# Attention scores in a hybrid decoder layer: q's high and low parts on the two row halves, two passes per head in place of three

## The chip, the core and the metric

The kernel runs on one core of one Trainium2 chip. The metric is the device time of one execution in microseconds (us); the time given for a kernel is the median of its runs. Rows of a trace come from one profiled execution, in us from the start of its span, and durations of single instructions are in ns where the row says so.

The engines are named as in the profile: PE is TensorE's matmul pipe and PEld its weight load, DVE is VectorE, ACT is ScalarE, POOL is GpSimd, SP is SyncE, which issues the weight loads from memory.

## What is computed

One decoder layer on 512 tokens of width 1024: a feed-forward block, a mixer of two branches on the same input (sliding-window attention with sinks, and a state-space scan), and a second feed-forward block, each followed by a layer norm. All in float32. The change touches the scores of the attention branch alone:

```python
qb = q.reshape(b, nb, ATTN_BLOCK, N_KV_HEADS, rep, HEAD_DIM)      # 4 blocks of 128 tokens, 4 x 4 heads of 64
kk, vv = with_prev(kb), with_prev(vb)                             # the block before, and the block itself
scores = jnp.einsum("bnqgrd,bnkgd->bngrqk", qb, kk).astype(jnp.float32) * (HEAD_DIM ** -0.5)
...
probs = jax.nn.softmax(jnp.concatenate([scores, sink], axis=-1), axis=-1)[..., :-1]
out = jnp.einsum("bngrqk,bnkgd->bnqgrd", probs.astype(v.dtype), vv)
```

The first block of tokens has no block before it, so it has 128 keys; the other three have 256.

## The kernel before

**Products of split numbers.** Nearly every matrix product is made of three TensorE passes. An operand is split into a high part (a copy rounded to fp32r, made by ACT) and a low part (the remainder, made by DVE from the original and the high part); `split_act` on lines 142 to 146 does this for activations and `split_w` on lines 96 to 102 for weights. `mm3` on lines 123 to 126 then runs high by high, high by low and low by high into one PSUM accumulator.

**Attention stage.** It lies between 400 and 560 us of the span. A list of 20 main tiles runs on PE: six tiles of q (`q_tile(2)` to `q_tile(7)`; the first two stand ahead of the list), six tiles of the scan's inputs, eight gate tiles. Each main tile is a product over 1024 inputs, 24 passes of 512 columns on the whole 128 x 128 array. `weave` (lines 374 to 392) puts one step of attention behind each main tile, which holds the scores of one unit, the values of the unit two before it and the turning of the probabilities of the unit one before it. A unit is one group of four heads (one key head) by one block of 128 tokens, so there are 16 units: 12 have 256 keys and 4 (the first block of each group) have 128.

**Scores.** `q_tile(i)` leaves two heads in one tile, head 0 on rows 0 to 63 and head 1 on rows 64 to 127, the high part and the low part side by side in the free dimension. `k_tile` (lines 436 to 444) puts high and low parts of each key head on both row halves, so that a head of q finds its keys on its own rows. In `scores`, line 476 runs `mm3` for each of the four heads on 64 rows: heads 0 and 2 on rows 0 to 63, heads 1 and 3 on rows 64 to 127, 12 passes a unit. The two halves write to two PSUM tiles (`pss`).

**Behind the scores.** DVE adds the band mask and takes the row maximum (line 478), ACT takes the exponential (line 485), DVE scales (line 491). PE turns the probabilities (line 500) and ACT and DVE split them (`pt`), PE multiplies by v (`values`).

**Order.** The order on each engine is made when the kernel is built: a scheduler places instructions by priority in the order of the code, and `issue_after` keeps attention's instructions behind the last pass of the main tile (`cur["mm"]`). Four PSUM buffers serve the main tiles (`acc`) and four the rest (`sm`). The q tiles have two buffers (`qT`, line 449): the tile of group 2 can be written only when the scores of group 0 are done, that of group 3 when those of group 1 are.

Of the kernel before, what the change touches and what calls it, by code (L numbers as in the profile page):

```python
# [12 lines left out]
ALU = mybir.AluOpType  # L13

P = 128
# [24 lines left out]
def hybrid_layer(  # L40
# [5 lines left out]
    nc = tc.nc  # L46
# [9 lines left out]
    def acc(name="acc"):  # L56
        return psum.tile([P, 512], F32, tag="acc", name=name)

    def sm(name="sm"):
        return psum.tile([P, 512], F32, tag="sm", name=name)  # L60

    def f(ap):
        return ap.bitcast(F32)
# [51 lines left out]
    def load_w(*srcs, pool=None, own=0):  # L115
        return split_w(*fetch_w(*srcs), pool=pool, own=own)

    def wcols(w, r0, nk, c0, n):
        return w[r0:r0 + nk * P, c0:c0 + n].rearrange("(k p) c -> p k c", p=P)

    cur = {}

    def mm3(ps, lh, ll, rh, rl, start, stop):
        nc.tensor.matmul(ps, lh, rh, start=start, stop=False)  # L124
        nc.tensor.matmul(ps, lh, rl, start=False, stop=False)  # L125
        cur["mm"] = nc.tensor.matmul(ps, ll, rh, start=False, stop=stop)  # L126

    def gemm_T(w, act, kk, col=0, ps=None, tok=slice(0, SEQ)):

        ps = ps or acc()  # L130
        wh, wl = w
        n = len(kk)
        for i, k in enumerate(kk):
            mm3(ps[:, tok], wh[:, i, col:col + P], wl[:, i, col:col + P], act[:, k, 0, tok], act[:, k, 1, tok], i == 0, i == n - 1)
        return ps
# [6 lines left out]
    def split_act(dst, ps):  # L142

        a = nc.scalar.copy(dst[0], ps)  # L144
        b = nc.vector.tensor_tensor(dst[1], ps, f(dst[0]), ALU.subtract)  # L145
        return a.ins, b.ins
# [115 lines left out]
    with tc.tile_pool(name="start", bufs=1) as pool:  # L262
# [7 lines left out]
        for k in range(8):  # L270
            ps = sm()
# [33 lines left out]
    with tc.tile_pool(name="mix", bufs=1) as mix:  # L305
# [89 lines left out]
        with tc.tile_pool(name="attn", bufs=1) as ap:  # L395
# [4 lines left out]
            for t in range(NT):  # L400
                ps = acc("vdt")
                tok = slice(t * P, (t + 1) * P)
# [29 lines left out]
            kT = ap.tile([P, NKV, 2, SEQ], F32R, name="kT")  # L432
            aT = ap.tile([P, 8, 2, SEQ], F32R, name="aT")
            qTs = {}
# [11 lines left out]
            def q_tile(i):  # L446
                g = i // 2
                if i % 2 == 0:
                    qTs[g] = ap.tile([P, 2, 2, SEQ], F32R, name="qT", bufs=2)
                ps = gemm_T(load_w(wcols(w_in, 0, 8, i * P, P)), xT, range(8))  # L450
                split_act((qTs[g][:, i % 2, 0], qTs[g][:, i % 2, 1]), ps)

            def attention():
                units = [(g, t) for g in range(NKV) for t in range(NT)]
                st = {}
                smls = ap.tile([P, 4, 8, 4], F32, name="smls")
                sinkB = smls[:, 3].rearrange("p a b -> p (a b)")[:, :16]
                nc.gpsimd.dma_start(sinkB, sinks[0].partition_broadcast(P))

                def scores(u):  # L460
                    g, t = u
                    tok = slice(t * P, (t + 1) * P)
                    nk = 1 if t == 0 else 2
                    ks = slice((t + 1 - nk) * P, (t + 1) * P)
                    pr = ap.tile([P, 4, 2 * P], F32, name="pr", bufs=2)
                    s3 = 4 * g + t
                    sml = smls[:, s3 % 3]
                    mx, nm, rs, es, rc = (sml[:, i] for i in range(5))
                    sink = sinkB[:, 4 * g:4 * g + 4]
                    bandv = band.rearrange("p a b -> p (a b)")[:, (2 - nk) * P:]  # L470
                    pss = [sm().rearrange("p (a b) -> p a b", a=2) for _ in range(2)]
                    for i in range(2):
                        for hh in range(2):
                            pp = slice(hh * 64, hh * 64 + 64)
                            q_, k_ = qTs[g][pp, i, :, tok], kT[pp, g, :, ks]
                            mm3(pss[hh][:, i, :nk * P], q_[:, 0], q_[:, 1], k_[:, 0], k_[:, 1], True, True)
                    for h in range(4):
                        nc.vector.tensor_tensor_reduce(
                            out=pr[:, h, :nk * P], in0=pss[h % 2][:, h // 2, :nk * P], in1=bandv, op0=ALU.add, op1=ALU.max,
                            scale=1.0, scalar=MASKED, accum_out=mx[:, h:h + 1])  # L480
                    nc.vector.scalar_tensor_tensor(nm, mx, 0.125, sink, ALU.mult, ALU.max)
                    nc.vector.tensor_tensor(es, sink, nm, ALU.subtract)
                    nc.vector.tensor_scalar_mul(nm, nm, -1.0)
                    for h in range(4):
                        nc.scalar.activation(pr[:, h, :nk * P], pr[:, h, :nk * P], AF.Exp, bias=nm[:, h:h + 1],  # L485
                                             scale=0.125, accum_out=rs[:, h:h + 1])
                    nc.scalar.activation(es, es, AF.Exp)
                    nc.vector.tensor_tensor(rc, rs, es, ALU.add)
                    nc.vector.reciprocal(rc, rc)
                    for h in range(4):  # L490
                        nc.vector.tensor_scalar_mul(pr[:, h, :nk * P], pr[:, h, :nk * P], rc[:, h:h + 1])
                    st[u] = (pr, nk)

                def turn(u):
                    pr, nk = st[u]
                    pts = []
                    for b in range(nk):
                        ps = sm()
                        for h in range(4):
                            nc.tensor.transpose(ps[:, h * P:(h + 1) * P], pr[:, h, b * P:(b + 1) * P], ident)  # L500
                        pt = ap.tile([P, 2, 4 * P], F32R, name="pt", bufs=3)
                        split_act((pt[:, 0], pt[:, 1]), ps)
                        pts.append(pt)
                    st[u] = pts

                def values(u):
                    g, t = u
                    pts = st.pop(u)
                    ps = sm()
                    nk = len(pts)  # L510
                    for b in range(nk):
                        v_ = vs[:, t + 1 - nk + b, :, g * HD:(g + 1) * HD]
                        mm3(ps[:HD], v_[:, 0], v_[:, 1], pts[b][:, 0], pts[b][:, 1], b == 0, b == nk - 1)
                    d = aT[:, 2 * g:2 * g + 2, :, t * P:(t + 1) * P]
                    pv = ps[:HD].rearrange("p (i j q) -> p i j q", i=2, j=2)
                    split_act((d[:HD, :, 0], d[:HD, :, 1]), pv[:, :, 0])
                    odd = ap.tile([HD, 2, P], F32R, name="odd", bufs=2)
                    split_act((odd, d[HD:, :, 1]), pv[:, :, 1])
                    nc.scalar.copy(d[HD:, :, 0], pv[:, :, 1])

                n = len(units)
                for s_ in range(n + 2):
                    if s_ < n:
                        scores(units[s_])
                    if 0 <= s_ - 2 < n:
                        values(units[s_ - 2])
                    if 0 <= s_ - 1 < n:
                        turn(units[s_ - 1])
                    yield
# [13 lines left out]

            k_tile(0)
            q_tile(0)
            ps = sm()
            dAf = dA.rearrange("p c h -> p (c h)")
# [4 lines left out]
            nc.scalar.activation(decf, ps[:, :384], AF.Exp)  # L552
            nc.vector.tensor_scalar_mul(decf[:, :256], decf[:, :256], 0.5)
            q_tile(1)
            k_tile(1)
            side = attention()
            mains = [lambda i=i: q_tile(i) for i in range(2, 8)] + xbc(0, mix)
            mains += [lambda j=j: gate_tile(j) for j in range(8)]
            weave(mains, side, 18, 0, 2)
# [207 lines left out]
```

## Time and profile before

| what | before |
|---|---|
| median of 3 runs | 1442.79 us (1442.69 to 1443.95) |
| profiled execution | 1442.51 us, of which the span is 1440.8 us |
| PE busy | 1417.8 us, 98% of the span, 6724 passes |
| weight load (PEld) busy | 1171.1 us, 81% |
| DVE busy | 782.3 us, 54% |
| ACT busy | 574.7 us, 40% |
| POOL busy | 108.9 us, 8% |
| mean granted TensorE clock | 0.998 of full speed |

Passes on PE are pipelined: a row of 0.39 us may follow the one before it by 0.23 us, and the end of a pass is modelled. What a pass costs in a stream is therefore the distance from its start to the next start, not its own duration. The page also gives the chain of work that ended last, with the share of each engine in it.

### The profile page before, as it was taken

The numbers are of one execution on the slowest core, as the hardware profiler recorded it, in microseconds if no ns is written. First come the engines' busy times: TensorE is split into PE (matmuls) and PEld (weight loads), VectorE is DVE, ScalarE is ACT, GpSimd is POOL, SyncE is SP. The second block draws the span as 40 slices with busy tenths as digits, with TensorE's granted clock in tenths as the row PEclk, the third lists the DMA queues.
The fourth block names the chain that finished last, engine by engine and source line by source line (L and its number), as shares of the span: only waits on it lengthen the run. The fifth ranks groups of instructions, "written<-read, shape, count | busy, mean of one in ns | idle before, by whom it ended". The sixth has DMA issues, their size and how long they took to land.

```text
span 1440.8 us, 17429 instructions
## 1 busy us (share of the span) xinstructions
PE 1417.8 (98%) x6724; PEld 1171.1 (81%) x6724; DVE 782.3 (54%) x1290; ACT 574.7 (40%) x1097; POOL 108.9 (8%) x150
## 2 busy tenths in 40 slices
PE   8999999999999999999999999999999999999997
PEld 6888888888877777888888888888888888888885
DVE  4433433233857985348758578577674343433235
ACT  4232232211346675258567467463223232232220
POOL 1000000000000000212101112031110000000001
PEclk9999999999999999999999999999999999999999
DMA  9433333233432223641432323335645333333221
GB/s 276 117 93 102 88 102 100 91 102 92 145 90 60 59 74 98 192 127 30 125 88 64 90 59 110 86 114 167 218 137 170 98 92 103 91 100 101 89 88 59
DMA packets 195636, 154.48 MB, mean 107 GB/s; under 512 B 6533, under 2 KB 169425, under 8 KB 195553
## 3 DMA queue, kind: packets, MB, share of 16 engines
q1 hardware_dynamic: 188608, 130.17, 30.3%
q0 software_dynamic: 6944, 23.19, 5.1%
q8 instruction: 53, 0.87, 0.2%
q14 instruction: 31, 0.25, 0.1%
HBM read 140.76 MB, written 12.58 MB: 106 GB/s over the span
## 4 chain that ended last, share of the span: by engine, by line
PE 90%; DVE 5%; ACT 3%; issue 1%; POOL 0%; DMA 0%; SPq 0%; DVEq 0%; ACTq 0%; POOLq 0%
PE acc L125 19%; PE acc L124 19%; PE acc L126 19%; PE dn L125 7%; PE dn L124 7%; PE dn L126 7%; PE sm L635 2%; PE z L125 1%; PE z L126 1%; PE z L124 1%; DVE wl L100 1%; ACT pr L485 1%; PE sm L124 1%; PE sm L126 1%; PE sm L125 1%
## 5 line engine op out<-in xcount | busy, mean ns | idle before, releaser
L99 ACT CAST wh<-raw 128x1024 fp32r<-128x1024 f32 (+1 forms) x233 | 244.0, 1050 | 653.0 <-issue 304.4
L100 DVE TENSOR_TENSOR wl<-raw,wh 128x1024 fp32r<-128x1024 f32 (+1 forms) x233 | 287.8, 1237 | 397.9 <-ACT wh L99 397.7
L124 PE MATMUL acc<-xT,wh 128*128 128x512 f32 (+2 forms) x1120 | 436.9, 390 | 0.0
L125 PE MATMUL acc<-xT,wh 128*128 128x512 f32 (+2 forms) x1120 | 434.4, 388 | 0.1
L126 PE MATMUL acc<-xT,wl 128*128 128x512 f32 (+2 forms) x1120 | 434.0, 388 | 0.0
L126 PEld LDWEIGHTS acc<-xT,wl 128*128 128x128 f32 x1120 | 210.3, 188 | 42.4
L124 PEld LDWEIGHTS acc<-xT,wh 128*128 128x128 f32 x1120 | 210.4, 188 | 42.0 <-ACT xT L144 0.2
L125 PEld LDWEIGHTS acc<-xT,wh 128*128 128x128 f32 x1120 | 210.5, 188 | 41.9 <-DVE xT L145 0.4
L124 PE MATMUL dn<-wh,hT 128*128 128x512 f32 x352 | 137.3, 390 | 0.0
L125 PE MATMUL dn<-wl,hT 128*128 128x512 f32 x352 | 137.2, 390 | 0.0
L126 PE MATMUL dn<-wh,hT 128*128 128x512 f32 x352 | 137.0, 389 | 0.0
L256 DVE TENSOR_TENSOR t<-t,acc 128x512 f32<-128x512 f32 x44 | 30.3, 688 | 111.6 <-PE acc L126 111.4
L591 ACT ACTIVATE ud<-upper,dAr 128x128 fp32r<-128x128 f32 x256 | 78.9, 399 | 2.7 <-DMA m1d<-ta 2.7
L126 PEld LDWEIGHTS dn<-wh,hT 128*128 128x128 f32 x352 | 66.1, 188 | 13.7
L124 PEld LDWEIGHTS dn<-wh,hT 128*128 128x128 f32 x352 | 66.1, 188 | 13.7
L125 PEld LDWEIGHTS dn<-wl,hT 128*128 128x128 f32 x352 | 66.1, 188 | 13.4
L160 POOL TENSOR_TENSOR sts<-sts,cols 128x1 f32<-128x1 f32 x12 | 11.9, 990 | 717.4 <-DVE sts L159 717.4
L124 PE MATMUL z<-wh,xT 128*128 128x512 f32 x128 | 50.2, 393 | 0.3 <-DVE CT L322 0.3
L124 PE MATMUL acc<-uT,wh 128*128 128x512 f32 x128 | 50.2, 392 | 0.0
L125 PE MATMUL z<-wl,xT 128*128 128x512 f32 x128 | 50.0, 390 | 0.0
L126 PE MATMUL z<-wh,xT 128*128 128x512 f32 x128 | 49.9, 390 | 0.0
L126 PE MATMUL acc<-uT,wl 128*128 128x512 f32 x128 | 49.9, 390 | 0.0
(228 smaller groups left out, 1726.1 us busy)
## 6 DMA issues: line engine op xcount, KB each, us to landing
raw<-in_w_in_dram SPq DMA_DIRECT2D x66, 512.0 KB, 3.7
raw<-in_ffn_w_gate_dram SPq DMA_DIRECT2D x44, 512.0 KB, 3.7
raw<-in_ffn_w_up_dram SPq DMA_DIRECT2D x44, 512.0 KB, 3.7
raw<-in_ffn_w_down_dram SPq DMA_DIRECT2D x44, 512.0 KB, 3.7
raw<-in_w_ssm_branch_dram SPq DMA_DIRECT2D x16, 512.0 KB, 3.5
raw<-in_w_attn_branch_dram SPq DMA_DIRECT2D x8, 512.0 KB, 4.1
raw<-in_w_out_dram SPq DMA_DIRECT2D x8, 512.0 KB, 4.4
r<-in_x_dram SPq DMA_DIRECT2D x8, 256.0 KB, 5.4
```

The source lines that it names most:

```text
L99: nc.scalar.copy(h[:, :n], raw[:, :n])
L100: nc.vector.tensor_tensor(l[:, :n], raw[:, :n], f(h[:, :n]), ALU.subtract)
L124: nc.tensor.matmul(ps, lh, rh, start=start, stop=False)
L125: nc.tensor.matmul(ps, lh, rl, start=False, stop=False)
L126: cur["mm"] = nc.tensor.matmul(ps, ll, rh, start=False, stop=stop)
L160: nc.gpsimd.tensor_tensor(mv[:, 3:4], mv[:, 2:3], mhalf[:, 0:1], ALU.pow)
L256: nc.vector.tensor_tensor(t, t, pu, ALU.mult)
L485: nc.scalar.activation(pr[:, h, :nk * P], pr[:, h, :nk * P], AF.Exp, bias=nm[:, h:h + 1], scale=0.125, accum_out=rs[:, h:h + 1])
L591: nc.scalar.activation(ud[:, i, h], upper, AF.Copy, scale=f(dAr[:, i, c, h0 + h:h0 + h + 1]))
L635: nc.tensor.matmul(py[:, h * HD:(h + 1) * HD], segs[h // 4][:, h % 4], xdt[:, h * HD:(h + 1) * HD], start=True, stop=True)
```

## The change

Per unit and head, three passes on 64 rows become one pass on 128 rows and one on 64. For this, q is laid out in another way: each head now has a plane of its own, with its high part on its own row half and its low part on the other half (line 449's shape stays 128 x 2 x 2 x 512, but the third dimension is now the head and no longer high or low). The pass on 128 rows multiplies the plane by the high part of the keys, which stands on both row halves, so it sums high by high and low by high. The pass on 64 rows adds q's high part by the low part of the keys.

```diff
@@ q_tile
-                split_act((qTs[g][:, i % 2, 0], qTs[g][:, i % 2, 1]), ps)
+                for hh in range(2):
+                    s_, o_ = slice(hh * 64, hh * 64 + 64), slice(64 - hh * 64, 128 - hh * 64)
+                    q_ = qTs[g][:, i % 2, hh]
+                    nc.scalar.copy(q_[s_], ps[s_])
+                    nc.vector.tensor_tensor(q_[o_], ps[s_], f(q_[s_]), ALU.subtract)
@@ scores
-                            q_, k_ = qTs[g][pp, i, :, tok], kT[pp, g, :, ks]
-                            mm3(pss[hh][:, i, :nk * P], q_[:, 0], q_[:, 1], k_[:, 0], k_[:, 1], True, True)
+                            q_, o = qTs[g][:, i, hh, tok], pss[hh][:, i, :nk * P]
+                            nc.tensor.matmul(o, q_, kT[:, g, 0, ks], start=True, stop=False)
+                            cur["mm"] = nc.tensor.matmul(o, q_[pp], kT[pp, g, 1, ks], start=False, stop=True)
```

PE, before, second unit (group 0, block 1): the last pass of the main tile, the first two heads (`sm_2900` is the PSUM tile of the heads on rows 0 to 63, `sm_2901` that of the heads on rows 64 to 127), six passes.

```order
L126 MATMUL acc_2872<-xT_92,wl_2869 128x512
L124 MATMUL sm_2900<-kT_2644,qT_2685 128x256
L125 MATMUL sm_2900<-kT_2644,qT_2685 128x256
L126 MATMUL sm_2900<-kT_2644,qT_2685 128x256
L124 MATMUL sm_2901<-kT_2644,qT_2685 128x256
L125 MATMUL sm_2901<-kT_2644,qT_2685 128x256
L126 MATMUL sm_2901<-kT_2644,qT_2685 128x256
```

The other two heads follow in the same way, and then the turning of the unit before (line 500). Three passes on the upper rows stand ahead of three on the lower rows.

PE, with the change, the same place (`sm_2904` and `sm_2905` are the two PSUM tiles; line 481 is the pass on 128 rows, line 482 the pass on 64, of rows 0 to 63 for `sm_2904` and of rows 64 to 127 for `sm_2905`).

```order
L126 MATMUL acc_2874<-xT_92,wl_2871 128x512
L481 MATMUL sm_2904<-kT_2644,qT_2685 128x256
L482 MATMUL sm_2904<-kT_2644,qT_2685 128x256
L481 MATMUL sm_2905<-kT_2644,qT_2685 128x256
L482 MATMUL sm_2905<-kT_2644,qT_2685 128x256
```

The other two heads follow in the same way, so a unit has eight passes in a row in which 128 rows and 64 rows alternate; each pass on 64 rows stands between two on 128. In one unit (the first block of group 2) a pass of the main tile stands between the second and the third head.

DVE, before, where the last two q tiles are split (`acc_3135` is `q_tile(6)`, `acc_3230` is `q_tile(7)`; `smls` and `pr` belong to softmax, `ct` to the scan's inputs).

```order
L478 ISA smls_2831 128x1
L491 TENSOR_SCALAR pr_3351<-pr_3351,smls_2831 128x256
L145 TENSOR_TENSOR qT_3128<-acc_3135,qT_3128 128x512
L145 TENSOR_TENSOR qT_3128<-acc_3230,qT_3128 128x512
L491 TENSOR_SCALAR pr_3351<-pr_3351,smls_2831 128x256 x3
L322 SCALAR_TENSOR_TENSOR ct_3441<-acc_3416,cols_90,ct_3441 128x511
```

DVE, with the change, the same place (`acc_3131` and `acc_3224` are the same two tiles).

```order
L497 TENSOR_SCALAR pr_3343<-pr_3343,smls_2837 128x256 x3
L456 TENSOR_TENSOR qT_3124<-acc_3131,qT_3124 64x512
L456 TENSOR_TENSOR qT_3124<-acc_3224,qT_3124 64x512
L497 TENSOR_SCALAR pr_3343<-pr_3343,smls_2837 128x256
L322 SCALAR_TENSOR_TENSOR ct_3429<-acc_3404,cols_90,ct_3429 128x511
L456 TENSOR_TENSOR qT_3124<-acc_3131,qT_3124 64x512
L456 TENSOR_TENSOR qT_3124<-acc_3224,qT_3124 64x512
L322 SCALAR_TENSOR_TENSOR ct_3429<-acc_3404,cols_90,ct_3429 128x510
```

Two instructions of 128 rows became four of 64 rows. No instruction moves on SP or POOL.

## Rows read from the trace of the kernel before

**Rows 1.** The page: busy time by engine, and clock in 40 slices.

```profile
PE 1417.8 (98%) x6724; PEld 1171.1 (81%) x6724; DVE 782.3 (54%) x1290; ACT 574.7 (40%) x1097; POOL 108.9 (8%) x150
...
PEclk9999999999999999999999999999999999999999
```

**Rows 2.** The page: chain that ended last, share of the span by engine.

```profile
PE 90%; DVE 5%; ACT 3%; issue 1%; POOL 0%; DMA 0%; SPq 0%; DVEq 0%; ACTq 0%; POOLq 0%
```

**Rows 3.** Windows, attention stage and its densest part: busy us (instructions) by engine.

```profile
417.00:562.00 145.00, 143.52 (x803) 109.81 (x802) 116.06 (x379) 98.36 (x263) 2.71 (x5) 1.00 0.26 72
...
466.00:507.00 41.00, 40.08 (x228) 29.72 (x227) 36.91 (x112) 29.36 (x74) 0.00 (x0) 1.00 0.20 52
```

**Rows 4.** Timeline of PE, second unit: start, duration, instruction, rows*columns of the array.

```profile
424.01 0.39 PE L125 MATMUL acc<-xT,wh 128*128 128x512 f32 x1
424.24 0.39 PE L126 MATMUL acc<-xT,wl 128*128 128x512 f32 x1
424.56 0.39 PE L124 MATMUL sm<-kT,qT 64*128 64x256 f32 x2
424.78 0.28 PE L125 MATMUL sm<-kT,qT 64*128 64x256 f32 x2
424.90 0.28 PE L126 MATMUL sm<-kT,qT 64*128 64x256 f32 x2
425.02 0.29 PE L124 MATMUL sm<-kT,qT 64*128 64x256 f32 x2
425.13 0.29 PE L125 MATMUL sm<-kT,qT 64*128 64x256 f32 x2
425.25 0.29 PE L126 MATMUL sm<-kT,qT 64*128 64x256 f32 x2
425.47 0.65 PE L500 MATMUL sm<-ident,pr 128*128 128x128 f32 x4
```

**Rows 5.** Groups of PE by shape: the scores' passes, count, busy us and mean ns.

```profile
L125 PE MATMUL sm<-kT,qT 64*128 64x256 f32 x48 | 6.9, 278 | 0.0
...
L125 PE MATMUL sm<-kT,qT 64*128 64x128 f32 x16 | 2.6, 272 | 0.0
```

**Rows 6.** Timeline of PEld: weight loads in a dense stream, then in the second unit.

```profile
419.71 0.19 PEld L125 LDWEIGHTS acc<-xT,wh 128*128 128x128 f32 x1
419.94 0.19 PEld L126 LDWEIGHTS acc<-xT,wl 128*128 128x128 f32 x1
...
424.56 0.19 PEld L124 LDWEIGHTS sm<-kT,qT 64*128 64x128 f32 x2 [0.35 <-issue]
424.67 0.20 PEld L125 LDWEIGHTS sm<-kT,qT 64*128 64x128 f32 x2
...
425.47 0.42 PEld L500 LDWEIGHTS sm<-ident,pr 128*128 128x128 f32 x4
```

**Rows 7.** Timeline of PE, a unit of 128 keys and the values behind it.

```profile
448.91 0.39 PE L126 MATMUL acc<-xT,wl 128*128 128x512 f32 x1
449.23 0.33 PE L124 MATMUL sm<-kT,qT 64*128 64x128 f32 x2
449.39 0.28 PE L125 MATMUL sm<-kT,qT 64*128 64x128 f32 x2
...
449.84 0.28 PE L126 MATMUL sm<-kT,qT 64*128 64x128 f32 x2
450.05 0.45 PE L124 MATMUL sm<-pt,vs 128*64 128x512 f32 x1
...
451.25 0.39 PE L126 MATMUL sm<-pt,vs 128*64 128x512 f32 x1
451.48 1.38 PE L500 MATMUL sm<-ident,pr 128*128 128x128 f32 x8
```

**Rows 8.** Groups, 395 to 562 us: ACT and DVE on q's and k's tiles; idle before them last.

```profile
L442 DVE TENSOR_TENSOR kT<-acc,kT 64x512 fp32r<-64x512 f32 x4 | 2.7, 685 | 0.8 <-ACT kT L441 0.8
L145 DVE TENSOR_TENSOR qT<-acc,qT 128x512 fp32r<-128x512 f32 x8 | 5.3, 687 | 0.4 <-ACT qT L144 0.4
L441 ACT CAST kT<-acc 64x512 fp32r<-64x512 f32 x4 | 2.3, 576 | 0.0
L144 ACT CAST qT<-acc 128x512 fp32r<-128x512 f32 x8 | 4.5, 584 | 0.1
```

**Rows 9.** Groups, 395 to 562 us: the weight load ahead of the turning passes, idle before it last.

```profile
L500 PEld LDWEIGHTS sm<-ident,pr 128*128 128x128 f32 x112 | 13.1, 140 | 8.9 <-DVE smls L478 3.0 <-ACT wh L99 1.0 <-ACT xn L343 0.9
```

## The prediction, made before the change was run

> **What bounds the kernel now.** I read the page first: PE is busy for 98% of the span at full clock in all 40 slices [rows 1], and PE has 90% of the chain that ended last [rows 2]. PE sets the time. Next the windows of the attention stage, 417 to 562 us: PE is busy for 143.5 of 145 us there, DVE for 116.1. In its densest part, 466 to 507 us, DVE has 36.9 of 41 us, nearly a second bound [rows 3]. So time added to PE's stream in this stage goes to the end almost whole, unless it fills a wait for DVE. How PE spends a unit of scores is seen in the timeline, and there the starts count, since the passes are pipelined.
>
> **Reading a unit of 256 keys.** The rows of the scores read "x2": a pass for rows 0 to 63 and one for rows 64 to 127 start together. Two passes of about 278 ns each [rows 5] fit into a stretch of 0.28 to 0.29 us, which they could not if one followed the other [rows 4]. Although the code has three passes of one half ahead of three of the other, the chip runs the halves side by side: 12 passes are six steps. From the second row to the sixth they are (425.25 - 424.78) / 4 = 0.1175 us apart. A dense pass of 512 columns takes 0.23 us (424.01 to 424.24).
>
> At the edges of the unit there is more to pay. From the last 128-row pass to the first 64-row pass it is 0.32 us, 0.09 over its own 0.23: I call this 0.09 the change of rows. From the last 64-row step to the next 128-row pass it is 0.22, 0.10 over its own 0.1175. And the first step is 0.22 long where the others are 0.1175, since its weight load starts at the same 424.56 as the pass: 0.10 of load is exposed. In a dense stream the next load starts with the pass before it (0.23 apart) and costs nothing [rows 6]. So a pass of another row count costs 0.09 to 0.10 for the change and 0.10 for its load, about 0.20 together. The unit occupies PE from 424.47 (424.24 + 0.23) to 425.47, 1.00 us.
>
> That it is the row count shows in the values: there 64 columns follow 64 rows, then 128 columns follow 64 columns at the ordinary 0.23 (451.25 to 451.48), with nothing extra [rows 7].
>
> The Trainium skill, "TensorEngine Tiling (Array Packing)", section Tiling Modes, Key Properties, says that changing the tiling mode, not just the tile, drains TensorE, and that different tiles load and multiply in parallel. It gives no figure. The trace agrees on both, with the 0.09 to 0.10 us and the "x2" rows. By this rule the changed unit drains eight times where the old one drained twice; without it the sum would be that of the first rival.
>
> **What the change does to PE.** It takes 64 of 192 passes away (four per unit, 16 units). But those were run side by side; now each 64-row pass stands between two 128-row passes, so none has a partner, and a unit has eight steps instead of six, with eight changes of rows instead of two. The first 128-row pass follows other 128-row passes and has its load hidden: 0.12 + 0.095 for the change behind it. Each of the other seven costs 0.10 (load) + 0.1175 + 0.095 (change behind it) = 0.31. Sum: 0.21 + 7 x 0.31 = 2.38 us against 1.00, so +1.38 for each of 12 units.
>
> A unit of 128 keys now goes from 449.14 (448.91 + 0.23) to 450.05, 0.91 us; its steps are 0.11 apart although they have half the columns, so there the load sets the pace [rows 7]. Alone, such a pass costs 0.11 (load) + 0.05 (the rest of the first step's 0.16) + 0.10 = 0.26, and the unit 0.15 + 7 x 0.26 = 1.97 us: +1.06 for each of 4 units.
>
> Sum: 12 x 1.38 + 4 x 1.06 = 16.6 + 4.2 = **+20.8 us on PE**.
>
> **What it does to ACT and DVE.** A q tile had one ACT copy (584 ns) and one DVE subtraction (687 ns) on 128 rows; now it has two of each on 64 rows. The k tiles show what 64 rows cost: 576 and 685 ns, the same [rows 8]. So ACT gets 8 x 0.58 = 4.6 us more and DVE 8 x 0.69 = 5.5 us. The trace has no subtraction of q that writes to the other row half; I take the same 0.69, and a gain or a longer one has no row. Each DVE half waits for its ACT half, and queued behind it are softmax's maxima, its scaling and the scan's `ct` steps, for which PE's turning passes wait. The cover is PE's own growth: in 466 to 507 us, where DVE is fullest, two q tiles are split (1.4 us more on DVE), while PE's five units there grow by 4 x 1.38 + 1.06 = 6.6 us. DVE's share falls rather than rises, so I cost it at nothing; without the cover it would be 1.4 us there, 5.5 at the most. SP and POOL get nothing, no transfer moves.
>
> **What PE's waits give back.** Ahead of the turning passes the weight load sits idle, of which 3.0, 1.0 and 0.9 us end with DVE or ACT [rows 9]. The turning of a unit stands behind the scores of the next one. These are now 1.4 us longer, so softmax has that much more time, and these waits shrink. Bounds: 0 (the scheduler has shifted some turning passes, and the waits could stay) to 4.9 us. I take 2.5, the middle, since a part of this idle time lies under passes still in flight.
>
> **The number.** 20.8 - 2.5 = +18.3 us. On the profiled execution's 1442.5 us this is 1460.8; it stands 0.3 below the median of 1442.8, so **1461 us**, 1.3% slower.
>
> **Rivals.**
> 1. A lone 64-row pass between 128-row passes pays neither change nor load, because it uses a part of the array that is set up already. Then a unit of 256 keys takes 8 x 0.1175 = 0.94 us against 1.00 plus 0.10 for the exposed load of the next pass, and one of 128 keys 8 x 0.11 = 0.88 against 1.01: 12 x -0.16 + 4 x -0.13 = -2.4, **1440 us**. For it: the trace has no such lone pass. Against it: all edges of the units shown pay. It is faster than before only if a change costs under 0.16 / 8 = 0.02 us, a tenth of what the edges show.
> 2. The load of the other row count is fetched ahead, and only the change of 0.095 is paid: 0.94 + 8 x 0.095 = 1.70 for 256 keys, 0.88 + 0.76 = 1.64 for 128. Against 1.10 and 1.01 this is 12 x 0.60 + 4 x 0.63 = +9.7, less 2.5 or so: **1450 us**. For it: dense passes load ahead. Against it: in the unit's first row, load and pass start together.
> 3. DVE's or ACT's new halves land where PE waits, and the old waits stay: 20.8 + 1.4 = 22.2, and with all 5.5 us of DVE 26.3: **1465 to 1469 us**. For it: DVE's 90% in the densest part. Against it: PE grows by more than DVE there.
>
> **How the numbers follow.** Forecast 0.74, rival 1 0.06, rival 2 0.10, rival 3 0.10. The forecast's own range is 1458.5 to 1463.6 by the waits alone (4.9 or 0 us), and some 1.1 us more on either side because the rows are read to 0.01 us (16 x 7 = 112 lone passes). The range of 1450 to 1467 takes in rival 2 and the nearer part of rival 3. A measurement of this kernel can tell about 0.2% (2.9 us) from no change: slower by more than that are the forecast and rivals 2 and 3, 0.94, of which I leave 0.01 to what I haven't seen: 0.93; within it lies most of rival 1, 0.05; faster 0.02.
>
> **What would show it.** In the timeline of the changed kernel, score passes no longer come in twos; each is about 0.31 us behind the one before it with 256 keys, 0.26 with 128, and its weight load starts with it. A unit of 256 keys takes about 2.4 us, and the attention stage is 18 to 21 us longer while the rest of the span keeps its length. The groups of q's tile have 16 instructions of 0.58 and 0.69 us. The idle time ahead of the turning passes is smaller. I am wrong if lone passes are 0.12 apart (rival 1) or 0.21 apart (rival 2), or if new idle time on PE ends with DVE's halves of q (rival 3).

## The result and the profile after

The changed kernel takes 1459.3 us (median of 4 runs, 1458.45 to 1460.57) against 1442.74 us before (4 runs): a ratio of 1.0114, 95% interval 1.0103 to 1.0126, or 16.6 us more. The forecast was 1461 us.

The profiled execution of after took 1460.57 us with a span of 1458.9, the slowest of its four runs. Here are the page's engine rows and its chain by engine, which answer to [rows 1, 2].

```profile
PE 1436.6 (98%) x6660; PEld 1183.4 (81%) x6660; DVE 788.8 (54%) x1298; ACT 579.0 (40%) x1105; POOL 108.9 (7%) x150
...
PEclk9999999999999999999999999999999999999999
...
PE 94%; DVE 2%; issue 1%; ACT 1%; POOL 0%; DMA 0%; SPq 0%; DVEq 0%; POOLq 0%; ACTq 0%
```

There are 64 passes fewer, and PE is busy for 18.8 us more. DVE and ACT have lost more than half of their part in the chain (from 5 and 3% to 2 and 1%): PE sets the time even more than before.

The span is 18.1 us longer than that of before, but about 2 us of it have nothing to do with the change. They arise in the first 20 us, where the input arrives. The first dense pass of the first tile, in before and then in after, by the timelines of PE:

```profile
12.15 0.48 PE L124 MATMUL acc<-xT,wh 128*128 128x512 f32 x1
```

```profile
13.14 0.77 PE L124 MATMUL acc<-xT,wh 128*128 128x512 f32 x1
```

It comes 1.0 us later and its record is longer. When both kernels are laid side by side pass by pass, the same dense pass is 2.0 us late from 20 us on and stays so until the attention stage, is 18.1 us late at the end of that stage, and 18.1 us late at the end of the span. So the stage lost 16.1 us, near the medians' 16.6, and nothing outside it moved.

The timeline of PE in after, the second unit, answers to [rows 4]:

```profile
427.07 0.39 PE L125 MATMUL acc<-xT,wh 128*128 128x512 f32 x1
427.30 0.39 PE L126 MATMUL acc<-xT,wl 128*128 128x512 f32 x1
427.52 0.28 PE L481 MATMUL sm<-kT,qT 128*128 128x256 f32 x1
427.73 0.38 PE L482 MATMUL sm<-kT,qT 64*128 64x256 f32 x1
428.04 0.38 PE L481 MATMUL sm<-kT,qT 128*128 128x256 f32 x1
428.36 0.38 PE L482 MATMUL sm<-kT,qT 64*128 64x256 f32 x1
...
429.60 0.38 PE L482 MATMUL sm<-kT,qT 64*128 64x256 f32 x1
429.92 0.33 PE L506 MATMUL sm<-ident,pr 128*128 128x128 f32 x1
```

No row of the scores reads "x2" any more. The first pass, of 128 rows as the dense pass ahead of it, follows at the ordinary 0.22 us. The next, of 64 rows, comes 0.21 later, and from there each is 0.31 to 0.32 behind the one before it. The unit goes from 427.52 to 429.91 (the start of the load below): 2.39 us, where before it took 1.00. The weight loads of the same stretch answer to [rows 6]:

```profile
427.30 0.19 PEld L481 LDWEIGHTS sm<-kT,qT 128*128 128x128 f32 x1
427.73 0.18 PEld L482 LDWEIGHTS sm<-kT,qT 64*128 64x128 f32 x1 [0.24 <-issue]
428.04 0.19 PEld L481 LDWEIGHTS sm<-kT,qT 128*128 128x128 f32 x1
...
429.91 0.20 PEld L506 LDWEIGHTS sm<-ident,pr 128*128 128x128 f32 x2
```

The load of the first 128-row pass starts with the dense pass ahead of it (427.30), as in a stream. Each later load starts only with its own pass (427.73, 428.04): nothing was loaded ahead over a change of rows. A unit of 128 keys answers to [rows 7]:

```profile
420.01 0.22 PE L481 MATMUL sm<-kT,qT 128*128 128x128 f32 x1
420.16 0.33 PE L482 MATMUL sm<-kT,qT 64*128 64x128 f32 x1
420.42 0.33 PE L481 MATMUL sm<-kT,qT 128*128 128x128 f32 x1
...
421.69 0.32 PE L482 MATMUL sm<-kT,qT 64*128 64x128 f32 x1
421.95 0.50 PE L124 MATMUL acc<-xT,wh 128*128 128x512 f32 x1
```

Its first step is 0.15, the others are 0.25 to 0.26, and the unit takes 1.94 us. Last, the windows of the stage and of its densest part, which answer to [rows 3], and then, from the groups, the weight load ahead of the turning passes (to [rows 9]) and the two halves of q's split (to [rows 8]):

```profile
419.00:580.00 161.00, 161.00 (x738) 120.88 (x737) 121.09 (x385) 100.98 (x269) 2.71 (x5) 1.00 0.23 64
473.00:520.00 47.00, 47.00 (x215) 34.69 (x214) 38.86 (x120) 30.54 (x78) 0.00 (x0) 1.00 0.18 47
```

```profile
L506 PEld LDWEIGHTS sm<-ident,pr 128*128 128x128 f32 x112 | 13.6, 140 | 3.5 <-DVE smls L484 0.2
...
L456 DVE TENSOR_TENSOR qT<-acc,qT 64x512 fp32r<-64x512 f32 x16 | 10.8, 686 | 2.3 <-ACT qT L455 1.9
L455 ACT CAST qT<-acc 64x512 fp32r<-64x512 f32 x16 | 9.0, 581 | 6.8 <-DVE qT L456 3.7 <-PE sm L482 2.8
```

PE is busy for 161.0 of 161 us in the stage. The idle time ahead of the turning passes has shrunk from 8.9 to 3.5 us, and of what DVE and ACT ended 0.2 is left. DVE's share of the densest part fell from 90% (36.9 of 41) to 83% (38.9 of 47). Each half of q's split lasts as long as a whole one did.

### The profile page after: what moved, and what is told of

Read it like the earlier page. It is cut to its first block, busy times and chain, and to the rows that moved or that the text cites. A ratio compares the mean times of both kernels' runs of the same rounds, so it can differ in the third digit from the quotient of the medians.

```text
span 1458.9 us, 17315 instructions
## 1 busy us (share of the span) xinstructions
PE 1436.6 (98%) x6660; PEld 1183.4 (81%) x6660; DVE 788.8 (54%) x1298; ACT 579.0 (40%) x1105; POOL 108.9 (7%) x150
## 4 chain that ended last, share of the span: by engine, by line
PE 94%; DVE 2%; issue 1%; ACT 1%; POOL 0%; DMA 0%; SPq 0%; DVEq 0%; POOLq 0%; ACTq 0%
PE acc L124 20%; PE acc L125 20%; PE acc L126 20%; PE dn L126 6%; PE dn L124 6%; PE dn L125 6%; PE sm L641 2%; PE z L126 1%; PE z L125 1%; PE z L124 1%; PE sm L482 1%; PE sm L481 1%; PE sm L124 1%; PE sm L506 1%; PE sm L126 1%
```

## The experiments

Four questions stood behind the sum: whether the halves really ran side by side, whether the changes of rows make the loss (and not the 128-row passes or the new layout), what q's split in halves costs, and what gives time back.

Laid side by side with before pass by pass, as above, the attention stage alone is longer by 7.1 us with one half, by 0.0 and 4.6 in the two other orders of the passes, by -2.2 with all passes on 128 rows, by 2.9 with the split alone, 19.6 with the extra passes, 20.0 with both, and 1.3 with the heads in another order. The first 20 us differ by 0.4 to 2.0 us from before, though nothing was changed there. So the differences of the medians below are those of the stage.

### Was the overlap of the halves real? One half alone

```diff
-                            pp = slice(hh * 64, hh * 64 + 64)
+                            pp = slice(0, 64)
```

> The kernel before with all 12 score passes of a unit on rows 0 to 63 (the odd heads are computed from the even heads' rows, so their scores are left out). Two changes of rows as before, but no pass has a partner on the other row half. Theory (the halves really run side by side): six more steps of 0.1175 us in 12 units and of 0.11 in 4, +8.5 + 2.6 = +11.1 us on PE, less 2 to 4.6 us of waits: 1449.5 to 1452.5 us. Rival (the overlap in the records is not real, the passes already follow each other): 1443 us.

Measured: 1449.99 us against 1443.18, ratio 1.0046 (1.0031 to 1.0061), +6.8 us. The first passes of the second unit and the one behind it, in the timeline of PE:

```profile
425.61 0.38 PE L124 MATMUL sm<-kT,qT 64*128 64x256 f32 x1
425.83 0.28 PE L125 MATMUL sm<-kT,qT 64*128 64x256 f32 x1
425.95 0.28 PE L126 MATMUL sm<-kT,qT 64*128 64x256 f32 x1
...
427.02 0.28 PE L126 MATMUL sm<-kT,qT 64*128 64x256 f32 x1
427.22 0.55 PE L500 MATMUL sm<-ident,pr 128*128 128x128 f32 x3
```

The step is still 0.12 us, but there are twelve. The pairs were real: without them the same number of passes with the same two changes is dearer. A unit of 256 keys takes 1.71 us in place of 1.00, one of 128 keys 1.58 in place of 0.91. One unit of 128 keys, the first block of group 2, grew by only 0.28, because in before it had run in nine steps already (timeline of PE in before, its first pass and the pass behind it):

```profile
484.85 0.32 PE L124 MATMUL sm<-kT,qT 64*128 64x128 f32 x1
...
486.06 0.44 PE L124 MATMUL sm<-pt,vs 128*64 128x512 f32 x1
```

That is 1.21 us from start to start, where the unit of [rows 7] has 0.82. So it is 12 x 0.71 + 3 x 0.67 + 0.28 = 10.8 us on PE, of which 4.0 did not reach the end.

### Do the changes of rows make the loss? The same passes in two other orders

The first order, called the sandwich, has two changes of rows a unit: two 128-row passes, four 64-row passes with partners, two 128-row passes.

```diff
...
+                    def full(i, first):
+                        for hh in range(2):
+                            cur["mm"] = nc.tensor.matmul(pss[hh][:, i, :nk * P], qTs[g][:, i, hh, tok], kT[:, g, 0, ks], start=first, stop=not first)
+                    def half(i, first):
+                        for hh in range(2):
+                            pp = slice(hh * 64, hh * 64 + 64)
+                            nc.tensor.matmul(pss[hh][:, i, :nk * P], qTs[g][pp, i, hh, tok], kT[pp, g, 1, ks], start=first, stop=not first)
+                    full(0, True)
+                    half(0, False)
+                    half(1, True)
+                    full(1, False)
```

> The changed kernel with the same eight score passes per unit in another order: 128-row passes of heads 0 and 1, then the four 64-row passes (heads 0 and 1, then 2 and 3, neighbours on different row halves), then the 128-row passes of heads 2 and 3. Theory (changes of rows and lost pairs make the loss): two changes instead of eight and the 64-row passes in pairs, a unit of 256 keys takes 4 x 0.1175 + 2 x 0.1175 + 2 x 0.2 = about 1.0 us plus nothing at its end, total 1441 us (1439 to 1444). Rival (the 128-row passes on the new plane, or q's new split on ACT and DVE, make the loss): order does not matter, 1457 to 1461 us.

Measured: 1443.18 us against 1443.16, ratio 0.9998 (0.9988 to 1.0007). The third unit in the timeline of PE and the pass behind it (behind the second unit PE waits for DVE):

```profile
432.90 0.40 PE L479 MATMUL sm<-kT,qT 128*128 128x256 f32 x2
433.23 0.50 PE L484 MATMUL sm<-kT,qT 64*128 64x256 f32 x4
433.66 0.50 PE L479 MATMUL sm<-kT,qT 128*128 128x256 f32 x2
434.00 0.39 PE L124 MATMUL sm<-pt,vs 128*64 128x512 f32 x1
```

The same eight passes on the same operands, in another order, take all 16 us back. The unit takes 1.10 us, from 432.90 to 434.00, and the last two 128-row passes take 0.34 of it: the first of them stands behind a change of rows, so its load is not fetched ahead. The expectation's own terms add up to 1.1 too (0.47 + 0.235 + 0.4), not to the 1.0 that it names. Before, the unit took 1.00 and left 0.05 to 0.10 of exposed load to the pass behind it (a first pass of the values takes 0.28 there and not 0.23, a dense pass 0.33). So this order gains nothing on PE, and 1443 in place of 1441 needs no other cause. In three of the 16 units, moreover, the 64-row passes ran without a partner on the other half.

The second order has four changes: two 128-row passes, two 64-row passes, and the same again.

```diff
                     for i in range(2):
                         for hh in range(2):
+                            nc.tensor.matmul(pss[hh][:, i, :nk * P], qTs[g][:, i, hh, tok], kT[:, g, 0, ks], start=True, stop=False)
+                        for hh in range(2):
+                            pp = slice(hh * 64, hh * 64 + 64)
+                            cur["mm"] = nc.tensor.matmul(pss[hh][:, i, :nk * P], qTs[g][pp, i, hh, tok], kT[pp, g, 1, ks], start=False, stop=True)
...
```

> The changed kernel with the passes in pairs: 128-row passes of heads 0 and 1, 64-row passes of heads 0 and 1, the same for heads 2 and 3. Four changes of rows a unit instead of eight, and the 64-row passes have partners. Theory (each change costs about 0.2 us with its load): a unit of 256 keys takes 0.33 + 0.31 + 0.43 + 0.31 = 1.38 us, about 0.49 more than the sandwich order with its free end, 7 us in all, less up to 3 us of waits: 1447 to 1450.5 us. Rival (only the lost partners cost, changes do not add up): as the sandwich order, 1443 us.

Measured: 1448.02 us, ratio 1.0031 (1.0020 to 1.0043). Rows of the second unit and of the pass behind it:

```profile
425.77 0.40 PE L479 MATMUL sm<-kT,qT 128*128 128x256 f32 x2
426.10 0.39 PE L482 MATMUL sm<-kT,qT 64*128 64x256 f32 x2
426.41 0.50 PE L479 MATMUL sm<-kT,qT 128*128 128x256 f32 x2
426.84 0.39 PE L482 MATMUL sm<-kT,qT 64*128 64x256 f32 x2
427.16 0.74 PE L506 MATMUL sm<-ident,pr 128*128 128x128 f32 x4
```

1.39 us, between the sandwich's 1.10 and the 2.39 of the change. Against 1.10 that is 0.29 more, and 0.05 to 0.10 for the load of the pass behind it. The expected 0.49 took the sandwich's unit as 1.0, which is 0.1 too little. In three units of this order, too, 64-row passes ran alone. With two, four and eight changes the totals are 1443.2, 1448.0 and 1459.3, and the undisturbed units 1.10, 1.39 and 2.39: the changes add up, and lost partners add to them.

### Are passes on 128 rows cheap when nothing changes? All eight on 128 rows

```diff
-                            cur["mm"] = nc.tensor.matmul(o, q_[pp], kT[pp, g, 1, ks], start=False, stop=True)
+                            cur["mm"] = nc.tensor.matmul(o, q_, kT[:, g, 1, ks], start=False, stop=True)
```

> The changed kernel with the second pass on 128 rows too (the same plane of q times the low part of the keys, which stands on both row halves; this adds the product of the two low parts). No pass of another row count is left. Theory: eight passes of 0.1175 us for 256 keys, 0.94 us, and no exposed load behind them: 16 x -0.15 = -2.4 us against before, 1440 us (1438.5 to 1443). Rival (q's new split is part of the loss, or passes on 128 rows cost more than on 64): 1445 us or more.

Measured: 1441.1 us against 1443.16, ratio 0.9985 (0.9975 to 0.9994). This is 18 us faster than the change and the fastest kernel of this study, by 2 us. The first and the last passes of the second unit:

```profile
425.86 0.28 PE L481 MATMUL sm<-kT,qT 128*128 128x256 f32 x1
425.97 0.28 PE L482 MATMUL sm<-kT,qT 128*128 128x256 f32 x1
426.09 0.28 PE L481 MATMUL sm<-kT,qT 128*128 128x256 f32 x1
...
426.69 0.28 PE L482 MATMUL sm<-kT,qT 128*128 128x256 f32 x1
427.39 0.92 PE L506 MATMUL sm<-ident,pr 128*128 128x128 f32 x4 [0.42 <-DVE pr L497]
```

Every pass is 0.12 behind the one before it. A pass that multiplies twice as many rows as it needs costs less than half of a lone 64-row pass. In this unit PE then waits 0.42 us for DVE's scaling: with so short a unit, softmax is waited for.

### What does q's split in halves cost? With and without longer work on PE

First the kernel before with only the split changed:

```diff
-                split_act((qTs[g][:, i % 2, 0], qTs[g][:, i % 2, 1]), ps)
+                for hh in range(2):
+                    s_ = slice(hh * 64, hh * 64 + 64)
+                    split_act((qTs[g][s_, i % 2, 0], qTs[g][s_, i % 2, 1]), ps[s_])
```

> The kernel before with only q's split done in halves of 64 rows (two ACT copies and two DVE subtractions a tile, each to its own rows, layout as before). Theory: ACT's 4.6 us and DVE's 5.5 us more lie beside PE's stream, 1442.7 us within 1.5. Rival (they land where PE waits): +1.4 to +5.5 us, 1444 to 1448 us.

Measured: 1446.31 us, ratio 1.0022 (1.0013 to 1.0032), +3.1 us. My theory failed here and the rival held. The weight load ahead of the turning passes, from 395 to 590 us, idle before it last:

```profile
L502 PEld LDWEIGHTS sm<-ident,pr 128*128 128x128 f32 x112 | 13.3, 140 | 11.7 <-DVE smls L480 4.7 <-ACT wh L99 1.1 <-PE sm L126 1.1
```

It was 8.9 us before [rows 9] and is 11.7 now; what ends with DVE's maxima grew from 3.0 to 4.7. Without longer work on PE, 3.1 us come through of the 10 us that the split adds to ACT and DVE together. How much of it is due to each of the two was not taken apart.

Then the kernel before with six extra dense passes ahead of the scores of each unit, their result unused:

```diff
+                    for _ in range(6):
+                        nc.tensor.matmul(pss[0].rearrange("p a b -> p (a b)"), xT[:, 0, 0, tok], xT[:, 0, 0], start=True, stop=True)
```

> The kernel before with six more dense passes of 128 rows and 512 columns ahead of the scores of each unit, into a PSUM tile that the scores then overwrite (their result is not used). PE gets 16 x 6 x 0.2265 = 21.7 us more work with nothing else changed. Theory (PE's waits for softmax in this stage, some 4.6 us, are filled by any longer work on PE): +17.1 us, 1459.8 us (1458 to 1462). Rival (the waits went away because of the changed order or q's new split): +21.7 us, 1464.4 us.

Measured: 1462.7 us, ratio 1.0134 (1.0119 to 1.0149), +19.5 us: between the two. Of 21.7 us some 2.2 were given back, not 4.6. The longest wait left is one of 1.30 us (timeline of PE):

```profile
500.73 0.63 PE L502 MATMUL sm<-ident,pr 128*128 128x128 f32 x4 [1.30 <-DVE smls L480]
```

Here two groups of turning passes stand one right behind the other (the group before ends its record at 499.43). By the profile the second was released by DVE's maxima, and those stand on DVE among the scan's `ct` steps of some 0.74 us each. That this order arose from the extra passes is my reading, not shown. What is shown is that longer work on PE need not give back every wait.

Both together:

> The kernel before with both the six extra dense passes of 128 rows ahead of each unit (result unused) and q's split in halves of 64 rows. It tells whether longer work on PE hides the split, which alone cost 3.1 us. Theory (hidden): as with the extra passes alone, 1462.7 us within 1. Rival (the split costs the same whatever PE does): 1465.8 us.

Measured: 1463.09 us, ratio 1.0137 (1.0122 to 1.0152), 0.4 us over the extra passes alone. The same split that cost 3.1 us by itself is hidden when PE has 1.4 us more to do per unit. The changed kernel likewise has more to do on PE, and hardly a wait for DVE is left there.

### How far ahead does a partner start? The heads in another order

```diff
-                    for i in range(2):
-                        for hh in range(2):
+                    for hh in range(2):
+                        for i in range(2):
```

> The kernel before with the code's order of the heads changed: the six passes of heads 0 and 2 (rows 0 to 63), then the six of heads 1 and 3 (rows 64 to 127). Theory (a pass on the other row half is taken from the queue although six passes stand ahead of it): 1443 us, within 1. Rival (only near neighbours run side by side): the passes of one half run alone, up to 12 steps a unit, +4 to +9 us, 1447 to 1452 us.

Measured: 1444.55 us, ratio 1.0008 (0.9998 to 1.0017). The total lies between the two, but the timeline of PE decides, second unit:

```profile
425.33 0.38 PE L124 MATMUL sm<-kT,qT 64*128 64x256 f32 x1
425.55 0.28 PE L125 MATMUL sm<-kT,qT 64*128 64x256 f32 x1
425.67 0.28 PE L126 MATMUL sm<-kT,qT 64*128 64x256 f32 x1
425.68 0.39 PE L124 MATMUL sm<-kT,qT 64*128 64x256 f32 x2
425.90 0.28 PE L125 MATMUL sm<-kT,qT 64*128 64x256 f32 x2
426.02 0.28 PE L126 MATMUL sm<-kT,qT 64*128 64x256 f32 x2
426.14 0.28 PE L124 MATMUL sm<-kT,qT 64*128 64x256 f32 x1
```

The row at 425.68 joins two passes. A window of the same timeline that ends at 425.70 has the first of them alone:

```profile
425.68 0.39 PE L124 MATMUL sm<-kT,qT 64*128 64x256 f32 x1
```

It starts 0.01 us behind the third pass, where passes of one half are 0.12 apart, and its record is as long as that of the first pass of a unit: it is the seventh pass, the first on rows 64 to 127. The fourth follows 0.11 later. So two passes run alone, the third has the seventh beside it, and behind the fourth come two pairs and three passes alone: nine steps in place of six. In all 16 units the seventh pass starts beside the third. Both theories are wrong as put: a partner was taken from four places ahead (from three in the kernel before), but not from five or six, since the first two passes ran alone. What set this limit is not shown; the seventh pass also waits for a semaphore, as the first pass of the second half does in the kernel before.

The units of 256 keys are 0.34 us longer than before, those of 128 keys 0.28, and the one of group 2, which had nine steps already, is 0.1 shorter: 12 x 0.34 + 3 x 0.28 - 0.1 = 4.8 us on PE, of which 1.4 reached the end: 3.4 were given back.

## Why the prediction was right

**The bound** was PE, and PE's stream in the stage was lengthened. This held; after the change the chain is PE's to 94%.

**The unit of 256 keys** was put at 2.38 us and is 2.39; single steps at 0.31, measured 0.31 to 0.32. **The unit of 128 keys** was put at 1.97 and is 1.94. The forecast read one unit of 128 keys and took the other three as like it. The first block of group 2 was not: it took 1.30 us before (1.21 and the 0.09 of its change of rows) and 1.95 after, without the main pass that stands in it. So the gross growth is 12 x 1.39 + 3 x 1.03 + 0.65 = 20.4 us, against 20.8 forecast. The price of a lone pass, worked out from the two edges of a unit before, held for all seven. Rival 1 (nothing to pay, 0.12) and rival 2 (load fetched ahead, 0.21) are out by these rows, and the totals with two, four and eight changes confirm it by time.

**ACT and DVE at nothing** was right for the changed kernel, and so was the reason given, PE's own growth as the cover: with it the split costs 0.4 us, without it 3.1, inside the bounds of 1.4 to 5.5 named for a lost cover. What I had not seen is that without such growth there is no cover: the split alone, in the kernel before, costs 3.1 us. With it the cost was measured in the kernel before with extra passes, not in the changed kernel itself, whose low parts go to the other row half (686 ns each, as without that). Rival 3 is out too: the idle time ahead of the turning passes fell, and none of it is seen to end with q's halves.

**What the waits give back** is the term that was mis-sized: 2.5 us taken, with bounds of 0 and 4.9; by the medians it was 20.4 - 16.6 = 3.8, by the stage alone 20.4 - 16.1 = 4.3, and no wait for softmax of any size is left on PE. I took the middle because part of the idle time seemed to lie under passes in flight. Most of it was real. One half alone gave back 4.0 and the heads in another order 3.4, where PE was lengthened in the same place, ahead of the turning passes; but the six extra passes, which stand there too, gave back only 2.2. How much comes back in which order is thus not explained. Of the 1.7 us between 1461 forecast and 1459.3 measured, 1.3 are this term and 0.4 the unit of group 2.

## What to carry to other kernels

Before passes are merged or their number is cut, look whether they run side by side: passes that start together are one step, and the steps count, not the passes. (A row with "x2" need not be such a pair: it can also join passes that follow each other, and then it lasts longer than one of them.) Passes of different row counts should stand in blocks, or be padded to the same rows: here eight padded passes beat both eight mixed ones, by 18 us, and twelve narrow ones, by 2. And where PE waits a little for softmax, longer work on PE is partly free (2.2 to 4.0 us here), so the waits belong into the price of a loss on PE.

## What the runs showed of the hardware

- A 64-row pass behind a 128-row one, or the other way round, starts about 0.1 us late and with a load that was not fetched ahead: 0.31 us for a lone pass of 256 columns, 0.12 in a stream of the same row count. A change in the number of columns used (64 to 128) costs nothing extra [rows 7]. And not every change of rows costs something: the one pass on 96 rows (line 288) starts 0.23 us behind the 128-row pass ahead of it (66.88 to 67.11 us in before), as in a stream.
- Passes on the two row halves are not started in the order of the code. The fourth pass of a unit starts with the first [rows 4], the seventh with the third when the code has six passes of one half ahead of six of the other; the longest reach seen is four places, and five and six were not reached there.
- With 128 columns to stream, passes of 64 rows follow each other by 0.11 us, hardly faster than with 256 (0.12) [rows 7]. So the columns do not set the pace there; that the weight load does is inferred, not tested.
